# Turning the next expert's tokens two slabs earlier, and taking the low-part products last, in a float32 mixture-of-experts block

## The chip, the core and the metric

The kernel runs on one core of a Trainium2 chip. The time is the device time of one execution in microseconds, as the median of several runs; lower is better. PE is the matrix engine (PEld its weight loads), ACT the scalar engine, DVE the vector engine, POOL the general engine and SP the engine that issues most transfers.

## The reference

One layer of a streaming encoder on 1024 tokens of 1024 channels: a mixing half (gated DeltaNet heads beside sparse attention heads), then a routed mixture of experts. The change touches the experts alone. What they compute, cut to its core:

```python
logits = h @ router_w + router_b                  # 1024 tokens, 32 experts
top_val, top_idx = lax.top_k(logits, 4)
gate = softmax(top_val)
def block_ffn(xb, e):                             # the tokens of expert e
    act = clamped_swiglu(xb @ w1[e] + b1[e])      # 1024 x 2048
    return act @ w2[e] + b2[e]                    # 1024 x 1024
out[tok] += gate * block_ffn(h[tok], e)
```

All of it is float32.

## The kernel before

PE multiplies in a rounded float32 format. To keep float32 precision each operand is split: the high part is a cast to that format (ACT, L193), the low part is the operand less its high part (DVE, L194). A product is then three: high times high, high tokens times low weights, low tokens times high weights.

**Slabs and halves.** An expert's weights come in 12 slabs of 1 MB (s = 0 to 7 for the first matrix, 8 to 11 for the second), fetched by SP into a ring of nine. Each slab is split in two halves, so that an expert has 24 halves. They live in rings of nine tiles, `hi0` to `hi8` and `lo0` to `lo8`. The split runs five halves ahead of the slab that PE is at (`LOOK`).

**Tokens.** `gather` brings up to 128 tokens of an expert, chosen by an indirect transfer on POOL, into `xg`. `transpose_x` turns them: eight transposes on PE into two PSUM tiles, two copies on ACT for the high part of `xT` (L1623), two subtractions on DVE for the low part (L1624). The first block of an expert (`first`) takes 128 tokens; where an expert has more, a second block (`both`) takes the rest, either in full or, for 64 tokens or fewer, in a narrow form that puts high and low parts side by side (`half`, `transpose_half`, L1631 to L1634). Which of them runs is decided on the chip by two Ifs (L1532, L1533).

**Order.** The loop over experts goes through the slabs in groups of two (s0 = 0, 2, ..., 10). For a group the program names the splits, the first block's pieces with what follows them (`behind`: activation, turning of the activation into `aT`, the result `y`), and then the If with the second block's pieces. The tokens of expert e + 1 are turned in the group s0 = 10, between that group's splits and its pieces. A scheduling layer sets the final order of each engine between two Ifs: it may lift first-block work of later groups ahead of an If, and in fact lifts all of groups 8 and 10 ahead of the If of s0 = 8 but for eight products. An engine executes in that order; no instruction passes one that waits.

In this text a stretch is what stands between two Ifs, named after the If that ends it. Stretch 0 goes from the If of s0 = 10 of one expert to the If of s0 = 0 of the next, so that it holds the end of one expert and the beginning of another; stretch 2 goes from there to the If of s0 = 2, and so on to stretch 8. The splits of a stretch are four (eight in stretch 0), in the order of the halves.

**A piece** (`piece`, L1664) is one slab against one block: two halves of two 128-row steps each, three products per step, 12 in all, in the order high-high, high-low, low-high for each step.

Of the kernel before, what the change touches and what calls it, by code (L numbers as in the profile page):

```python
# [20 lines left out]
P = 128  # L21
# [6 lines left out]
NE = 32  # L28
# [108 lines left out]
class K:  # L137
# [1305 lines left out]
    def phase4(self):  # L1443
        nc, tc, A, pp = self.nc, self.tc, self.A, self.pp
        ET = mybir.EngineType
        with ExitStack() as es:
# [33 lines left out]
            def split(g):  # L1480
                if g < 2 * NE * NS:
                    self.split_ring(g)
                    if g % 2:
                        self.fetch(g // 2 + NR)
# [5 lines left out]
            def gather(b, e):  # L1490
                if e < NE:
                    self.gather(self.xg[b], ix(b, e))

            def path_of(e):
                return [nc.values_load(path[0:1, e:e + 1], engines=on, min_val=0, max_val=2)
                        for on in ((ET.PE, ET.Activation, ET.DVE), (ET.Pool,))]
# [8 lines left out]
            for e in range(NE):  # L1505
                several, pool = paths
                paths = path_of(e + 1) if e + 1 < NE else None
                pick = lambda h: self.sel[:, h, e:e + 1].to_broadcast([P, P])
                wt = lambda g: (self.hi[(2 * e * NS + g) % NW], self.lo[(2 * e * NS + g) % NW])
                first = Block(self, 0, P, self.xg[0], self.xT, pick, ga(0, e), self.y0)  # L1510
                xT1 = st.tile([P, 2, KD, P], F32R, name="xT1")
                both = Block(self, 1, P, self.xg[1], xT1, pick, ga(1, e), y1)
                half = both.half(lambda h: self.selh[:, h])

                for s0 in range(0, NS, GP):
                    group = range(s0, s0 + GP)
                    for s in group:
                        for part in range(2):
                            split(2 * (e * NS + s) + part + LOOK)
                    if s0 == 2:  # L1520
                        gather(1, e + 1)
                    if s0 == 10 and e + 1 < NE:
                        self.transpose_x(self.xg[0], self.xT)
                        gather(0, e + 2)
                    for s in group:
                        first.room(s)
                        first.piece(s, wt)
                        first.behind(s)

                    for s in group:  # L1530
                        both.room(s)
                    with tc.If(several > 0):  # L1532
                        with tc.If(several > 1) as many:  # L1533
                            if s0 == 0:
                                self.transpose_x(self.xg[1], xT1)
                            for s in group:
                                both.piece(s, wt)
                                both.behind(s)
                        with many.Else():
                            if s0 == 0:  # L1540
                                self.transpose_half(self.xg[1], half.X)
                                for h in range(2):
                                    nc.scalar.copy(self.selh[:, h, 0:64], self.sel[:, h, e:e + 1].to_broadcast([P, 64]))
                            for s in group:
                                half.piece(s, wt)
                                half.behind(s)
                self.add_rows(self.y0, ix(0, e), P)
                with tc.If(pool > 0):  # L1548
                    self.add_rows(y1, ix(1, e), P)
# [57 lines left out]
    def gather(self, xg, ix):  # L1607

        self.nc.gpsimd.indirect_dma_start(out=xg, out_offset=None, in_=self.dH[:, :],  # L1609
                                          in_offset=bass.IndirectOffsetOnAxis(ap=ix, axis=0), bounds_check=T - 1, oob_is_err=False)  # L1610
# [26 lines left out]
class Block:  # L1637
# [26 lines left out]
    def piece(self, s, wt):  # L1664
        nc, z = self.k.nc, self.z
        if s < 8:
            ps, X, h = self.rooms[s], self.X, s % 2
            if h == 0:
                c0 = 512 * (s // 2)
                nc.tensor.matmul(ps, self.pick(c0 // 1024), self.k.bias[:, c0 % 1024:c0 % 1024 + 512], start=True, stop=False,  # L1670
                                 skip_group_check=True)
            first = False
        else:
            ps, X, h = self.rooms[s], self.aT, (s - 8) // 2
            first = h == 0
        mm = lambda l, r, start, stop: nc.tensor.matmul(ps, l, r, start=start, stop=stop, skip_group_check=True)  # L1676
        for part in range(2):
            wh, wl = wt(2 * s + part)
            for j in range(2):
                k = 4 * h + 2 * part + j  # L1680
                begin, end = first and part == 0 and j == 0, h == 1 and part == 1 and j == 1
                if z == P:
                    mm(X[:, 0, k], wh[:, j], begin, False)
                    mm(X[:, 0, k], wl[:, j], False, False)
                    mm(X[:, 1, k], wh[:, j], False, end)
                else:
                    mm(X[:, k], wh[:, j], begin, False)
                    mm(X[:, k], wl[:, j], False, end)

    def behind(self, s):  # L1690

# [66 lines left out]
```

## Time and profile before

| | |
|---|---|
| time, median of 3 runs | 2689.1 us (2684.57 to 2692.34) |
| the profiled execution | 2686.3 us |
| its span, first to last instruction | 2684.6 us, 35831 instructions |
| PE busy | 2405.1 us (90%) |
| DVE busy | 1935.8 us (72%) |
| ACT busy | 1511.1 us (56%) |
| POOL busy | 599.2 us (22%) |
| read from memory, written | 534.89 MB, 54.57 MB |

The busy shares are averages over stages that differ. The experts begin about 1010 us after the start. PE's busy time contains pipelined products: one of 512 columns lasts about 0.39 us in the trace, while the next starts 0.23 us after it, so that the distance from start to start is what a product costs. The idle time in brackets in a timeline is counted from the end of the instruction before. "<-" names what ended it; PEq is PE's own sequencer.

### The profile page before, as it was taken

The page shows a single profiled execution, that of the slowest core. Times are in us where ns is not written, and L with a number is a line of the kernel's source. Part 1 is how long each engine was busy: PE and PEld are TensorE (multiplying, and loading weights), DVE is VectorE, ACT ScalarE, POOL GpSimd, SP SyncE. Part 2 cuts the span into 40 slices and gives each one's busy share as a digit, 9 for nine tenths or more (in the row PEclk, how much of TensorE's full clock was granted, in tenths as well). Part 3 has the DMA queues.
Part 4 walks back from the last instruction along what each step waited for, and adds up shares of the span by engine and source line. Part 5 has one row for each costly group of instructions (what it writes and reads, how often), then busy time and mean ns, then how long its engine had stood idle before and what let it go on. Part 6 is the DMA issues. An engine that isn't in the chain of part 4 may idle for free. (4 is left out here: it accounts for less than half of the span.)

```text
span 2684.6 us, 35831 instructions
## 1 busy us (share of the span) xinstructions
PE 2405.1 (90%) x11702; PEld 1914.4 (71%) x11702; DVE 1935.8 (72%) x3547; ACT 1511.1 (56%) x2449; POOL 599.2 (22%) x424
## 2 busy tenths in 40 slices
PE   5999989798897978999899989889999999999986
PEld 4877778787786756767677766666767777677765
DVE  6797896478875887886776676488888756775644
ACT  6558323267664325676665655467677646564533
POOL 0033321344532433121121120121221211121110
PEclk8999999889998979999999999999999999999998
DMA  8123345554414348896776675489999857784740
GB/s 316 48 80 133 110 164 195 166 135 126 116 47 180 120 157 299 315 336 240 272 281 239 232 284 195 170 295 335 334 328 329 315 181 265 252 308 183 268 146 12
DMA packets 144836, 570.66 MB, mean 213 GB/s; under 512 B 36820, under 2 KB 62452, under 8 KB 89252
## 3 DMA queue, kind: packets, MB, share of 16 engines
q1 hardware_dynamic: 111876, 496.33, 51.2%
q0 software_dynamic: 19792, 43.37, 6.4%
q10 hardware_dynamic: 12880, 27.30, 2.8%
q8 instruction: 159, 2.61, 0.4%
q14 instruction: 129, 1.06, 0.1%
HBM read 534.89 MB, written 54.57 MB: 220 GB/s over the span
## 5 line engine op out<-in xcount | busy, mean ns | idle before, releaser
L1676 PE MATMUL m<-hi,xT 128*128 128x512 f32 x2464 | 839.7, 406 | 90.3 <-DVE xT L1624 48.5
L1676 PEld LDWEIGHTS m<-hi,xT 128*128 128x128 f32 x2464 | 465.4, 193 | 243.3 <-DVE xT L1624 63.8
L194 DVE TENSOR_TENSOR lo<-raw,hi 128x1024 fp32r<-128x1024 f32 x436 | 509.8, 1220 | 104.0 <-ACT hi L193 102.3
L1676 PE MATMUL m<-lo,xT 128*128 128x512 f32 x1344 | 537.3, 400 | 0.1
L193 ACT CAST hi<-raw 128x1024 fp32r<-128x1024 f32 x436 | 428.9, 1046 | 114.4 <-PEq L1532 98.2
L194 DVE TENSOR_TENSOR lo<-yT,hi 128x1024 fp32r<-128x1024 f32 x340 | 398.0, 1220 | 68.4 <-ACT hi L193 68.4
L1676 PE MATMUL m<-hi,aT 128*128 128x512 f32 x1232 | 422.3, 406 | 6.6 <-ACT aT L1731 3.1
L193 ACT CAST hi<-yT 128x1024 fp32r<-128x1024 f32 x340 | 334.9, 1046 | 67.2 <-PEq L1532 61.1
L1609 POOL DMA_INDIRECT xg<-dH,L x63 | 79.7, 1265 | 999.3 <-PE tr L1621 963.1
L1676 PEld LDWEIGHTS m<-lo,xT 128*128 128x128 f32 x1344 | 257.8, 192 | 58.3 <-issue 0.8
L1676 PEld LDWEIGHTS m<-hi,aT 128*128 128x128 f32 x1232 | 226.9, 188 | 69.2 <-issue 12.2
L1613 POOL DMA_INDIRECT out_dram<-y,L x41 | 192.4, 4692 | 364.1 <-DVE y L1737 296.7
L1676 PE MATMUL m<-lo,aT 128*128 128x512 f32 x672 | 266.4, 396 | 7.3 <-DVE lo L194 7.3
L1717 ACT ACTIVATE act<-m,c 128x256 f32<-128x256 f32 x140 | 66.1, 472 | 245.1 <-PE m L1676 232.0
L200 PE MATMUL mm<-hTh,wh 128*128 128x512 f32 (+2 forms) x400 | 155.7, 389 | 2.0 <-ACT xpad L469 1.1
L202 PE MATMUL mm<-hTh,wl 128*128 128x512 f32 (+2 forms) x400 | 154.2, 385 | 0.0
L201 PE MATMUL mm<-hTl,wh 128*128 128x512 f32 (+2 forms) x400 | 154.2, 385 | 0.0
L1676 PEld LDWEIGHTS m<-lo,aT 128*128 128x128 f32 x672 | 126.5, 188 | 36.7 <-DVE lo L194 10.8
L1719 DVE TENSOR_SCALAR m<-m 128x256 f32<-128x256 f32 x140 | 59.8, 427 | 87.9 <-ACT act L1717 86.2
L1096 POOL TENSOR_TENSOR L<-Tb,mask 128x128 f32<-128x128 f32 (+3 forms) x64 | 85.9, 1342 | 159.1 <-PE tr L1135 116.8
L1708 DVE TENSOR_TENSOR y<-m,y 64x512 f32<-64x512 f32 x42 | 28.7, 682 | 127.4 <-ACT y L1707 127.4
L1707 ACT COPY y<-m 64x512 f32<-64x512 f32 x42 | 24.5, 582 | 151.8 <-PE m L1676 117.5
(461 smaller groups left out, 4171.0 us busy)
## 6 DMA issues: line engine op xcount, KB each, us to landing
raw<-in_w_dram SPq DMA_DIRECT2D x214, 1024.0 KB
yT<-in_w_dram SPq DMA_DIRECT2D x166, 1024.0 KB
raw<-in_mod_w_dram SPq DMA_DIRECT2D x24, 1024.0 KB
raw<-in_w_in_dram SPq DMA_DIRECT2D x16, 1024.0 KB
dU<-stage ACTq DMA_DIRECT2D x12, 512.0 KB
dT<-dF SPq DMA_DIRECT2D x8, 576.0 KB
x<-in_x_dram SPq DMA_DIRECT2D x8, 512.0 KB
dQK<-stage ACTq DMA_DIRECT2D x8, 512.0 KB
```

The costliest lines, as they stand in the source:

```text
L193: nc.scalar.copy(hi, raw)
L194: nc.vector.tensor_tensor(lo, raw, hi, op=ALU.subtract)
L200: nc.tensor.matmul(ps, xh(k), yh(k), start=(k == 0), stop=False)
L201: nc.tensor.matmul(ps, xh(k), yl(k), start=False, stop=False)
L202: nc.tensor.matmul(ps, xl(k), yh(k), start=False, stop=(k == n - 1))
L1096: nc.gpsimd.tensor_tensor(L[:, :n], Tb[:, t0:t0 + n], self.masks[b], op=ALU.add)
L1609: self.nc.gpsimd.indirect_dma_start(out=xg, out_offset=None, in_=self.dH[:, :], in_offset=bass.IndirectOffsetOnAxis(ap=ix, axis=0), bounds ...
L1613: self.nc.gpsimd.indirect_dma_start(out=self.out[:, :], out_offset=bass.IndirectOffsetOnAxis(ap=ix[:z], axis=0), in_=y[:z], in_offset=None ...
L1676: mm = lambda l, r, start, stop: nc.tensor.matmul(ps, l, r, start=start, stop=stop, skip_group_check=True)
L1708: k.nc.vector.tensor_tensor(u, ps[0:64], u, op=ALU.add)
L1717: nc.scalar.activation(r, ug, AF.Relu, bias=k.c7[:z, 0:1], scale=-1.0)
L1719: nc.vector.tensor_scalar(ul, ul, 7.0, -7.0, op0=ALU.min, op1=ALU.max)
```

## The change

Two edits. The turning of the next expert's tokens, with the gather for the expert after it, moves from the group s0 = 10, behind its splits, to the head of the group s0 = 8, ahead of that group's splits. And in a piece for 128 tokens the four products of a slab with the tokens' low parts come after the eight with the high parts; narrow blocks keep their order.

```diff
                 for s0 in range(0, NS, GP):
                     group = range(s0, s0 + GP)
+                    if s0 == 8 and e + 1 < NE:
+                        self.transpose_x(self.xg[0], self.xT)
+                        gather(0, e + 2)
                     for s in group:
                         for part in range(2):
                             split(2 * (e * NS + s) + part + LOOK)
                     if s0 == 2:
                         gather(1, e + 1)
-                    if s0 == 10 and e + 1 < NE:
-                        self.transpose_x(self.xg[0], self.xT)
-                        gather(0, e + 2)
                     for s in group:
...
-        for part in range(2):
-            wh, wl = wt(2 * s + part)
-            for j in range(2):
-                k = 4 * h + 2 * part + j
-                begin, end = first and part == 0 and j == 0, h == 1 and part == 1 and j == 1
-                if z == P:
-                    mm(X[:, 0, k], wh[:, j], begin, False)
-                    mm(X[:, 0, k], wl[:, j], False, False)
-                    mm(X[:, 1, k], wh[:, j], False, end)
-                else:
-                    mm(X[:, k], wh[:, j], begin, False)
-                    mm(X[:, k], wl[:, j], False, end)
+        ks = [(4 * h + 2 * part + j, *(t[:, j] for t in wt(2 * s + part)), first and part + j == 0, h + part + j == 3)
+              for part in range(2) for j in range(2)]
+        if z < P:
+            for k, wh, wl, begin, end in ks:
+                mm(X[:, k], wh, begin, False)
+                mm(X[:, k], wl, False, end)
+            return
+
+        for k, wh, wl, begin, end in ks:
+            mm(X[:, 0, k], wh, begin, False)
+            mm(X[:, 0, k], wl, False, False)
+        for k, wh, wl, begin, end in ks:
+            mm(X[:, 1, k], wh, False, end)
```

The scheduling layer moves more than the diff says. The pieces below are of one expert whose ring starts at `hi0`, so that `hi8` is the first split of stretch 6, `hi0` the second, and `hi3`, `hi4`, `hi5` the first three of stretch 8.

ACT in stretch 8 (the If of s0 = 6 behind it), before:

```order
L193 CAST hi3_8874<-raw1_8868 128x1024
L193 CAST hi4_8875<-raw2_8869 128x1024
L193 CAST hi5_8876<-raw2_8869 128x1024
L193 CAST hi6_8877<-raw3_8870 128x1024
L1731 CAST aT0_16778<-tr_17280 128x256
```

and of the change:

```order
L193 CAST hi3_8874<-raw1_8868 128x1024
L1623 CAST xT_10447<-tr_17244 128x512
L1623 CAST xT_10447<-tr_17251 128x512
L193 CAST hi4_8875<-raw2_8869 128x1024
L193 CAST hi5_8876<-raw2_8869 128x1024
L193 CAST hi6_8877<-raw3_8870 128x1024
L1732 CAST aT0_16778<-tr_17297 128x256
```

The two copies of the tokens stand behind the first split of stretch 8; before they stood behind the fourth of stretch 0. DVE has its two subtractions at the same place.

PE at the head of stretch 8, before (m0 are the first block's sums, m1 the second's, aT0 the first block's turned activation, act0 the activation itself):

```order
L1532 UNCONDITIONAL_BRANCH
L1676 MATMUL m0_17267<-hi0_8871,aT0_16778 128x512 x2
L1676 MATMUL m0_17267<-lo0_8865,aT0_16778 128x512
L1676 MATMUL m0_17267<-hi0_8871,aT0_16778 128x512
L1676 MATMUL m0_17267<-hi1_8872,aT0_16778 128x512
L1676 MATMUL m0_17267<-lo1_8866,aT0_16778 128x512
L1676 MATMUL m0_17267<-hi1_8872,aT0_16778 128x512 x2
L1676 MATMUL m0_17267<-lo1_8866,aT0_16778 128x512
L1676 MATMUL m0_17267<-hi1_8872,aT0_16778 128x512
L1727 MATMUL tr_17280<-ident_60,act0_17156 128x128 x2
L1676 MATMUL m0_17254<-hi2_8873,aT0_16778 128x512
L1676 MATMUL m0_17254<-lo2_8879,aT0_16778 128x512
```

and of the change:

```order
L1532 UNCONDITIONAL_BRANCH
L1621 MATMUL tr_17244<-ident_60,xg0_10391 128x128 x4
L1621 MATMUL tr_17251<-ident_60,xg0_10391 128x128 x4
L1676 MATMUL m0_17271<-lo2_8879,aT0_16778 128x512
L1676 MATMUL m0_17271<-hi2_8873,aT0_16778 128x512
L1676 MATMUL m0_17271<-lo2_8879,aT0_16778 128x512
L1670 MATMUL m0_17484<-bias_9602,sel_9603 128x512
L1728 MATMUL tr_17297<-ident_60,act0_17156 128x128 x2
L1676 MATMUL m0_17284<-hi4_8875,aT0_16778 128x512
L1676 MATMUL m0_17284<-lo4_8881,aT0_16778 128x512
L1676 MATMUL m0_17284<-hi4_8875,aT0_16778 128x512
L1676 MATMUL m0_17271<-hi3_8874,aT0_16778 128x512
```

The products of `hi0` and `hi1` have moved ahead of the If of s0 = 6. `hi4`, a split of this stretch, stands behind the transposes, three products and a bias row; before it stood behind 16 products.

PE at the head of stretch 6, before:

```order
L1532 UNCONDITIONAL_BRANCH
L1676 MATMUL m0_17142<-hi4_8875,xT_10447 128x512
L1676 MATMUL m0_17142<-hi5_8876,xT_10447 128x512
L1676 MATMUL m0_17142<-lo5_8882,xT_10447 128x512
L1676 MATMUL m0_17142<-hi5_8876,xT_10447 128x512 x2
L1676 MATMUL m0_17142<-lo5_8882,xT_10447 128x512
L1676 MATMUL m0_17142<-hi5_8876,xT_10447 128x512
L1676 MATMUL m0_17142<-hi6_8877,xT_10447 128x512
L1676 MATMUL m0_17142<-lo6_8883,xT_10447 128x512
L1676 MATMUL m0_17142<-hi6_8877,xT_10447 128x512 x2
L1676 MATMUL m0_17142<-lo6_8883,xT_10447 128x512
L1676 MATMUL m0_17142<-hi6_8877,xT_10447 128x512
```

and of the change:

```order
L1532 UNCONDITIONAL_BRANCH
L1676 MATMUL m0_17142<-hi5_8876,xT_10447 128x512
L1676 MATMUL m0_17142<-hi6_8877,xT_10447 128x512 x2
L1728 MATMUL tr_17173<-ident_60,act0_17044 128x128 x2
L1676 MATMUL m0_17271<-hi7_8878,aT0_16778 128x512
L1676 MATMUL m0_17271<-lo7_8884,aT0_16778 128x512
L1676 MATMUL m0_17271<-hi7_8878,aT0_16778 128x512
L1676 MATMUL m0_17271<-lo7_8884,aT0_16778 128x512
L1676 MATMUL m0_17271<-hi8_10444,aT0_16778 128x512
L1676 MATMUL m0_17284<-hi0_8871,aT0_16778 128x512
L1676 MATMUL m0_17271<-lo8_10445,aT0_16778 128x512
L1676 MATMUL m0_17271<-hi8_10444,aT0_16778 128x512
```

`hi8` and `hi0`, splits of this stretch, stand behind seven products and two transposes; before, `hi8` stood behind 19 products, of which the piece shows the first 13.

## Rows read from the trace of the kernel before

**Rows 1.** Waits of the whole span: us in total, times, longest us
```profile
...
PE m L1676 <- DVE xT L1624: 48.5, 31, 2.6
...
PE m L1676 <- ACT xT L1623: 26.3, 27, 2.1
```

**Rows 2.** The tile xT: count, ns min/median/max, first and last start
```profile
...
L1624 DVE TENSOR_TENSOR xT<-tr,xT x70: 669/682/692, 1012.2 to 2593.4; 128x512 fp32r<-128x512 f32 x70
L1633 ACT CAST xT<-tr x7: 578/585/587, 1232.3 to 2601.8; 128x512 fp32r<-128x512 f32 x7
```

**Rows 3.** Windows: length, busy (count) by engine, clock, DMA share, GB/s
```profile
...
1441.00:1486.00 45.00, 40.63 (x168) 30.77 (x167) 36.63 (x44) 29.38 (x39) 9.40 (x4) 0.92 0.84 290
1831.00:2117.00 286.00, 263.75 (x1149) 201.45 (x1148) 240.15 (x280) 201.66 (x266) 59.82 (x21) 1.00 0.92 333
```

**Rows 4.** Timeline of PE, start of an expert: start, us, instruction, [idle <-releaser]
```profile
...
1872.63 1.07 PE L1621 MATMUL tr<-ident,xg 128*128 128x128 f32 x8 [0.71 <-PEq L1532]
1873.45 0.72 PE L1676 MATMUL m<-hi,aT 128*128 128x512 f32 x2
...
1876.46 0.50 PE L1676 MATMUL m<-hi,xT 128*128 128x512 f32 x1 [0.67 <-ACT xT L1623]
...
1878.41 0.73 PE L1676 MATMUL m<-hi,xT 128*128 128x512 f32 x2 [1.21 <-DVE xT L1624]
```

**Rows 5.** Timeline of ACT, the same stretch
```profile
...
1875.84 1.06 ACT L1623 CAST xT<-tr 128x512 fp32r<-128x512 f32 x2
```

**Rows 6.** Timeline of DVE, the same stretch
```profile
...
1877.67 1.28 DVE L1624 TENSOR_TENSOR xT<-tr,xT 128x512 fp32r<-128x512 f32 x2
1878.87 1.40 DVE L1737 SCALAR_TENSOR_TENSOR y<-m,L,g2b 128x512 f32<-128x512 f32 x2
```

**Rows 7.** Timeline of PE, an expert's second products, no second block
```profile
...
1913.48 0.74 PE L1621 MATMUL tr<-ident,xg 128*128 128x128 f32 x5 [0.71 <-PEq L1532]
```

**Rows 8.** Timeline of ACT, the same stretch
```profile
...
1906.21 1.05 ACT L193 CAST hi<-yT 128x1024 fp32r<-128x1024 f32 x1 [1.95 <-PEq L1532]
1907.16 2.94 ACT L193 CAST hi<-raw 128x1024 fp32r<-128x1024 f32 x3
```

**Rows 9.** Timeline of DVE, the same stretch
```profile
...
1907.29 1.23 DVE L194 TENSOR_TENSOR lo<-yT,hi 128x1024 fp32r<-128x1024 f32 x1 [1.25 <-ACT hi L193]
1908.43 3.49 DVE L194 TENSOR_TENSOR lo<-raw,hi 128x1024 fp32r<-128x1024 f32 x3
```

**Rows 10.** Timeline of PE, an expert with a narrow second block
```profile
...
1414.61 0.73 PE L1676 MATMUL m<-hi,xT 128*128 128x512 f32 x2
```

**Rows 11.** Timeline of ACT, the same stretch
```profile
...
1416.78 2.93 ACT L193 CAST hi<-yT 128x1024 fp32r<-128x1024 f32 x3
```

**Rows 12.** Timeline of DVE, the same stretch
```profile
...
1417.85 2.36 DVE L194 TENSOR_TENSOR lo<-yT,hi 128x1024 fp32r<-128x1024 f32 x2 [0.52 <-ACT hi L193]
```

**Rows 13.** Timeline of PE, that expert, behind its first If
```profile
...
1391.59 0.63 PE L1676 MATMUL m<-hi,xT 128*128 128x512 f32 x2
```

**Rows 14.** Timeline of DVE, the same stretch
```profile
...
1396.33 0.42 DVE L1720 SCALAR_TENSOR_TENSOR act<-m,act 128x256 f32<-128x256 f32 x1
```

**Rows 15.** Timeline of PE, that expert's second products
```profile
...
1425.50 0.73 PE L1676 MATMUL m<-hi,aT 128*128 128x512 f32 x2
...
1431.15 0.49 PE L1676 MATMUL m<-lo,aT 128*128 128x512 f32 x1 [0.94 <-DVE lo L194]
1431.86 0.50 PE L1676 MATMUL m<-hi,aT 128*128 128x512 f32 x1 [0.22 <-ACT aT L1731]
```

**Rows 16.** Timeline of PE, start of the expert behind it
```profile
...
1441.74 1.03 PE L1621 MATMUL tr<-ident,xg 128*128 128x128 f32 x8
...
1447.01 0.80 PE L1676 MATMUL m<-hi,xT 128*128 128x512 f32 x1 [2.14 <-ACT xT L1623]
...
1449.80 1.22 PE L1676 MATMUL m<-hi,xT 128*128 128x512 f32 x2 [1.56 <-DVE xT L1624]
```

**Rows 17.** Timeline of DVE, the same stretch
```profile
...
1444.53 4.61 DVE L194 TENSOR_TENSOR lo<-raw,hi 128x1024 fp32r<-128x1024 f32 x4
```

## The prediction

> **What bounds the kernel now.** The experts begin at 1012 of the span's 2684.6 us [rows 2] and run to its end. I read first the windows: over the seven experts from 1831 to 2117 PE is busy 263.75 of 286 us with 1149 instructions, at clock 1.00 and a DMA share of 0.92 [rows 3]. So PE sets the pace, at 0.23 us from one instruction to the next, and an expert without second block takes 40.85 us (1872.63 to 1913.48, [rows 4, 7]). Then the waits: PE idles 48.5 us for the low parts of the next expert's tokens and 26.3 for their high parts, nearly once per expert each [rows 1]. The timelines show why. The turned tokens stand on ACT and DVE behind four splits, and PE has only eight products and a bias row to run before it needs them [rows 4 to 6]. Start to start, at 0.23 a product and some 0.08 more after a stall, this costs 0.86 us (1876.46 instead of 1875.60) and 1.41 (1878.41 instead of 1877.00): 2.2 us per expert. Behind an expert with a narrow second block the waits are 2.14 and 1.56, the clock of the next 45.0 us is 0.92 [rows 3, 16], and that expert takes 4.1 us more than the 40.85, so the same place costs 6.3 there, some 2.1 of it clock.
>
> There are 7 narrow second blocks (x7 of L1633) and 3 full ones (70 halves of tokens turned, 64 of them for first blocks) [rows 2]; 22 experts have none. The last expert is a narrow one and turns no further tokens.
>
> A fact that decides below: ACT and DVE start a stretch's four splits only when PE has left the If ahead of it ("<-PEq L1532" in [rows 8]). Without second block ACT starts with PE; behind a narrow block it starts 2.17 us after PE (1414.61 to 1416.78) and DVE 3.24 [rows 10 to 12], because it still finishes that block's activation.
>
> **The change, part by part.** Nothing is added: the same 8 transposes, 2 copies, 2 subtractions, the same 12 products per piece, one gather. The waits change place.
>
> *The turn at stretch 0 goes.* It takes away the 2.2 (or 6.3) us. What is late next there: DVE now runs one result and four low parts first. Without second block the first low part of the next weights is ready about 3.4 us into the stretch, PE asks at 3.5 (seven products left, then four): no wait. Behind a narrow block DVE is free at 1444.53 [rows 17]; one result (two take 1.40, [rows 6]) and a low part, 0.70 + 1.23, end at 1446.5, PE (from 1441.74, eleven products, one more) asks at 1444.7: a wait of 1.8 stays.
>
> *The turn at stretch 8, no second block.* Let ACT's first split begin at 0 [rows 8]. PE's transposes take 0.82 (1872.63 to 1873.45, [rows 4]). ACT: first split, then at 0.95 the two copies, 1.06 together [rows 5], so the second split ends at 2.01 + 1.05 = 3.06. DVE: first low part at 1.08, next start 1.14 later [rows 9], then the two token low parts, 1.28 [rows 6], so the second low part ends at 2.22 + 1.28 + 1.23 = 4.73. PE: 0.84 after the transposes, three products and a bias row 0.92, two transposes 0.25: at 2.0 it asks for the second split (hi4 in the order): wait 1.06. One product later, at 3.3, it asks for lo4: wait 1.44. Together 2.5 us where the trace has no wait at all on splits. The two matmul orders together show it: PE asks for the first half of the last slab (hi4) before the second half of the one before it (hi3), and nothing behind a waiting product passes it. All the products of the piece and the second block's If queue behind it. Bounds: nothing (PE has no such wait now) and 4.7 (the narrow case below). I take 2.5, since every duration in it is a row.
>
> *Low parts last, and the later Ifs.* The order hoists more products ahead of each If and asks each slab's second half two products earlier. So a stretch begins with fewer products of old weights, and PE reaches the stretch's own first split sooner: in stretch 6 after 7 products and two transposes instead of 19 products. Without second block that just fits (asked at about 2.0, ready at 1.1), except stretch 2, where the transposes of the activations stand behind 13 products instead of 22 and wait about 0.25. Behind a narrow block it doesn't fit. Stretch 6: asked at 1.95, ready at 2.17 + 1.05 = 3.22; the next split asked 0.23 later, ready at 4.17; the low part at 4.47: together 2.1. Stretch 4: asked at 2.65, ready 3.22; low part asked at 3.5, ready 4.47: 1.6. Stretch 2: the activation is ready at 1396.75, 5.16 after PE's start [rows 13, 14]; asked at 3.1: 2.1. Stretch 8: ACT's copies wait for PE's transposes, which need DVE's tail of the If; second split ends about 5.7, second low part about 7.0, asked at 2.3: 4.7. Now in stretch 8 lo4 is the 18th product, due at 4.3 and run at 5.65, and the next wait adds 0.4 [rows 15]: 1.8.
>
> *What costs nothing.* The gather of expert e + 2 goes out some 10 us earlier on POOL, ahead of the rows to be added, and both have an expert's time to land. SP's slab transfers are issued behind the splits; in stretch 8 the second split is 1.1 us later, which nine slabs of lead cover at a DMA share of 0.92; without that cover each would cost its 1.1. The order of additions in a piece changes no duration.
>
> **The sum**, in us against the profiled 2686.3 (span 2684.6, 1.7 around it):
> - 22 experts without second block: -2.2 + 0.25 + 2.5 = +0.5 each, +11.
> - 6 narrow ones: new 2.1 + 1.6 + 2.1 + 4.7 + 1.8 = 12.3, old 1.8 + 6.3 = 8.1: +4.2 each, +25. The last one, without turn: 2.1 + 1.6 + 2.1, about +6.
> - 3 full ones: between nothing and the narrow 4.2; nearer to nothing, since ACT has no copy to make there: +1 each, +3.
>
> +45, so 2731. The profiled execution lies 2.8 under the median of the runs, inside their spread of 7.8; I leave it at 2731.
>
> **Rivals.**
> - *The waits vanish.* The tokens are ready early and PE meets no new wait: 22 x 2.2 + 6 x 6.3 + 3 x 4 (estimate between the two) = 98 less, 2588. For it: the 75 us in [rows 1]. Against: [rows 8, 9] give the splits no room, and at 38.6 us an expert the DMA share 0.92 becomes 0.97. It decides if PE reaches hi4 and lo4 of stretch 8 more than 2.5 us later than I count. Chance 0.17.
> - *It cancels.* PE's longer stretches let DVE catch up, the narrow experts lose half of 4.2 and the others gain half a us: within 8 us of 2686. Chance 0.15.
> - *The clock falls at the new place.* In stretch 8 two waits come close together, behind transposes and four products. Where the clock falls now it costs 2.1 us more than the waits; at the 28 turns of experts with a narrow block or none this is 59 more: 2790. For it: [rows 3], 0.92 behind waits of 2.14 and 1.56. Against: the seven experts from 1831 wait 0.67 and 1.21 behind the same transposes at 1.00. Chance 0.12.
>
> The Trainium skill (TensorE: Matmul & The Clock Gate, "Part 4: PE-mode transpose") says that transposes don't count as busy time for the clock as products do. By that rule the head of stretch 8 would look idler than a row of products, and the time would go to the third rival's 2790; by the rows at 1.00, where the same transposes stand ahead of the waits, it stays at 2731.
>
> **How the numbers follow.** Forecast 0.56, rivals 0.17, 0.15, 0.12. About 0.3% (8 us) is what a measurement can tell from no change here. Slower: forecast and third rival, 0.68; same 0.15; faster 0.17. The likeliest case alone runs from 2700 (no second block -0.5 each, narrow +3 and +6, full 0) to 2755 (+1.5, +4.2 and +6, +1). The range goes down to 2678, the lower end of the second rival, and up to 2790, the third.
>
> **What would show it.** Right: waits of PE for xT gone, new ones "<-ACT hi" and "<-DVE lo" of about 1.1 and 1.4 at L1676 in aT products, once per expert, an expert without second block at 41 to 41.5 us, a narrow one 3 to 5 us longer than now with its successor. ACT's and DVE's busy times unchanged. Wrong: periods under 40.5 us, or waits on splits that stay under 1 us per expert; then PE's place in the order was misjudged. A clock under 1.00 in the windows of experts without second block would be the third rival.

## The result and the profile after

The change makes the kernel slower: 2757.3 us median (2749.34 to 2761.77, 4 runs) against 2687.5 (the kernel before, by now 4 runs), a ratio of 1.0255 with a 95% interval of 1.0225 to 1.0284. The forecast was 2731, in the range 2678 to 2790. The profiled execution of after is the lowest of its runs (2749.3 us, span 2747.6), so that the two profiles differ by 63.0 us of span where the medians differ by 69.7.

The waits of PE over the whole span of after (us in total, times, longest), which answer to [rows 1]:

```profile
PE m L1676 <- DVE lo L194: 47.2, 44, 1.8
PE tr L1728 <- DVE act L1721: 30.7, 10, 9.2
PE tr L1728 <- DVE xT L1624: 29.7, 31, 1.8
PE m L1676 <- ACT hi L193: 17.9, 26, 3.0
```

The 48.5 and 26.3 us for xT in products are gone but for 0.4. In their place PE waits for low and high parts of splits, and its transposes of the activations (L1728) wait for the subtractions of xT and, longer than before, for the activations themselves (30.7 us against 11.3).

To place the loss I took each expert from ACT's first split of its stretch 0 to that of the next expert. An expert without second block lasts 40.86 us before and 40.91 after (medians of the same seven experts): nothing gained, nothing lost. The six narrow experts with their successors cost 50.3 us more, 8.4 each; the three full ones 4.4 together; the last expert 8.7. That makes up the 63 (the rest cancels within half a us).

The windows of after show the same. First row: seven experts without second block, against [rows 3]; then stretches 2, 4, 6 and 8 of the narrow expert that begins at 1377.5; last, stretch 2 of another narrow expert. Columns as in [rows 3].

```profile
1872.50:2158.80 286.30, 263.81 (x1148) 200.75 (x1148) 240.09 (x280) 200.28 (x267) 59.21 (x21) 1.00 0.90 331
...
1397.10:1412.32 15.22, 13.06 (x52) 9.99 (x51) 7.80 (x13) 6.79 (x12) 0.00 (x0) 0.89 0.35 138
1412.32:1424.98 12.66, 11.38 (x48) 8.09 (x46) 7.13 (x11) 6.69 (x12) 0.00 (x0) 1.00 0.45 167
1424.98:1439.89 14.91, 12.29 (x49) 9.29 (x49) 7.13 (x11) 6.68 (x12) 0.00 (x0) 0.89 0.37 141
1439.89:1457.60 17.71, 14.82 (x59) 11.18 (x58) 7.55 (x10) 6.45 (x11) 1.00 (x1) 0.90 0.42 150
1518.80:1532.40 13.60, 11.45 (x52) 8.78 (x51) 7.80 (x13) 6.74 (x12) 0.00 (x0) 1.00 0.42 157
```

The same four stretches of the same expert in the kernel before:

```profile
1394.09:1405.66 11.57, 11.49 (x51) 8.85 (x50) 7.80 (x13) 6.80 (x12) 0.00 (x0) 1.00 0.48 182
1405.66:1416.75 11.09, 11.09 (x50) 8.73 (x49) 7.13 (x11) 6.69 (x12) 0.00 (x0) 1.00 0.51 191
1416.75:1427.64 10.89, 10.89 (x49) 8.53 (x48) 7.13 (x11) 6.68 (x12) 0.00 (x0) 1.00 0.50 194
1427.64:1442.43 14.79, 13.63 (x61) 10.08 (x61) 6.36 (x8) 5.47 (x9) 0.00 (x0) 1.00 0.38 143
```

With the same busy time on DVE in stretches 2 to 6, they are 3.65, 1.57, 4.02 and 2.92 us longer, and the clock is below 1.00 in three of them.

Stretch 8 of an expert without second block in after, PE (start, us, instruction, idle time and releaser), which answers to [rows 4, 7]:

```profile
1905.76 1.06 PE L1621 MATMUL tr<-ident,xg 128*128 128x128 f32 x8 [0.30 <-PEq L1532]
...
1908.55 0.44 PE L1728 MATMUL tr<-ident,act 128*128 128x128 f32 x2 [0.79 <-DVE xT L1624]
1908.74 0.48 PE L1676 MATMUL m<-hi,aT 128*128 128x512 f32 x1
1910.28 0.50 PE L1676 MATMUL m<-lo,aT 128*128 128x512 f32 x1 [1.05 <-DVE lo L194]
```

ACT and DVE in that stretch, which answer to [rows 5, 6, 8, 9]:

```profile
1905.59 1.05 ACT L193 CAST hi<-yT 128x1024 fp32r<-128x1024 f32 x1 [2.25 <-PEq L1532]
1906.54 1.07 ACT L1623 CAST xT<-tr 128x512 fp32r<-128x512 f32 x2
1907.50 2.95 ACT L193 CAST hi<-yT 128x1024 fp32r<-128x1024 f32 x3
```

```profile
1906.67 1.23 DVE L194 TENSOR_TENSOR lo<-yT,hi 128x1024 fp32r<-128x1024 f32 x1 [1.55 <-ACT hi L193]
1907.81 1.28 DVE L1624 TENSOR_TENSOR xT<-tr,xT 128x512 fp32r<-128x512 f32 x2
1909.01 3.49 DVE L194 TENSOR_TENSOR lo<-yT,hi 128x1024 fp32r<-128x1024 f32 x3
```

The activations' transposes need one of two PSUM tiles (`tr`), which the subtractions release; so PE stops there, ahead of the product of the second split. That split ends at about 1908.55 (1907.50 + 1.05), the moment at which PE goes on: without the tile, the split would have held it about as long.

Stretch 2 of the narrow expert in after, PE, which answers to [rows 13, 14]. Behind the wait a product follows the last by 0.43 us, not 0.23, the lower of the clock's two levels (1.2 instead of 2.4 GHz):

```profile
1397.35 0.39 PE L1676 MATMUL m<-hi,xT 128*128 128x512 f32 x1
1399.90 0.47 PE L1728 MATMUL tr<-ident,act 128*128 128x128 f32 x2 [2.16 <-DVE act L1721]
...
1400.60 0.63 PE L1676 MATMUL m<-hi,xT 128*128 128x512 f32 x1
1401.02 0.63 PE L1676 MATMUL m<-lo,xT 128*128 128x512 f32 x1
```

The same place in another narrow expert of the same execution, behind the same wait:

```profile
1518.98 0.39 PE L1676 MATMUL m<-hi,xT 128*128 128x512 f32 x1
1521.52 0.41 PE L1728 MATMUL tr<-ident,act 128*128 128x128 f32 x2 [2.15 <-DVE act L1721]
...
1522.00 0.39 PE L1676 MATMUL m<-hi,xT 128*128 128x512 f32 x1
1522.23 0.39 PE L1676 MATMUL m<-lo,xT 128*128 128x512 f32 x1
```

Here the clock stays up, and the stretch lasts 13.60 us instead of 15.22: one fall of the clock costs 1.6 us.

### The profile page after: what moved, and what is told of

The parts are those of the page before. It is cut to its first block, busy times and chain, and to the rows that moved or that the text cites. A ratio compares the mean times of both kernels' runs of the same rounds, so it can differ in the third digit from the quotient of the medians.

```text
span 2747.6 us, 35638 instructions
## 1 busy us (share of the span) xinstructions
PE 2421.4 (88%) x11702; PEld 1916.7 (70%) x11702; DVE 1933.7 (70%) x3547; ACT 1507.1 (55%) x2449; POOL 601.5 (22%) x424
## 3 DMA queue, kind: packets, MB, share of 16 engines
q14 instruction: 130, 1.06, 0.1%
## 4 chain that ended last, share of the span: by engine, by line
issue 55%; PE 8%; POOL 6%; DMA 5%; DVE 4%; ACT 1%; another core or an unknown queue 1%; POOLq 1%; SPq 0%; ACTq 0%; DVEq 0%
POOL xg L1609 3%; POOL out_dram L1613 2%; DMA out_dram<-y,L 1%; PE tr L1145 1%; DMA dL<-pair,rdest 1%; DMA xg<-dH,L 1%; PE big L202 1%; PE big L200 1%; PE big L201 1%; DVE Xb L931 1%; DMA raw<-in_w_out_dram 1%; PE tr L1135 1%; PE lg L1118 1%; DVE tb L929 1%
## 5 line engine op out<-in xcount | busy, mean ns | idle before, releaser
L1676 PE MATMUL m<-hi,xT 128*128 128x512 f32 x2464 | 829.5, 400 | 13.7 <-DVE xT L1634 6.8
L1676 PE MATMUL m<-lo,xT 128*128 128x512 f32 x1344 | 543.3, 405 | 23.9 <-DVE lo L194 17.5
L1676 PE MATMUL m<-hi,aT 128*128 128x512 f32 x1232 | 430.9, 414 | 35.7 <-ACT hi L193 15.1
L1676 PEld LDWEIGHTS m<-hi,aT 128*128 128x128 f32 x1232 | 237.6, 194 | 108.5 <-ACT hi L193 24.9
L1676 PE MATMUL m<-lo,aT 128*128 128x512 f32 x672 | 280.1, 417 | 29.7 <-DVE lo L194 29.7
L1609 POOL DMA_INDIRECT xg<-dH,L x63 | 86.6, 1375 | 755.1 <-PE tr L1621 702.5
```

## The experiments

All times are medians; ratios are against the kernel before on the same chip. "hi8" counts the first-block products that stand ahead of the first product of stretch 6's own first split in PE's order (the transposes of activations beside them). "next stretch" says that this product stands only behind the next If, and an empty field that it was not counted. "Plain" is the median of the seven experts without second block that begin at 1831 in the kernel before; "narrow" the mean of four narrow experts each with its successor.

| kernel | us | ratio, 95% interval | hi8 | plain | narrow |
|---|---|---|---|---|---|
| before | 2687.5 | 1 | 19 | 40.86 | 112.9 |
| the change | 2757.3 | 1.0255 (1.0225 to 1.0284) | 7 | 40.91 | 120.7 |
| turn_only | 2778.3 | 1.0335 (1.0303 to 1.0367) | 5 | 41.80 | 123.0 |
| low_last_only | 2716.8 | 1.0112 (1.0084 to 1.0140) | 12 | 40.90 | 115.8 |
| turn10_ahead | 2742.9 | 1.0190 (1.0156 to 1.0225) | 6 | 40.60 | 119.5 |
| after_trm0 | 2642.6 | 0.9831 (0.9805 to 0.9857) | next stretch | 40.68 | 107.9 |
| turn_only_trm0 | 2638.1 | 0.9814 (0.9791 to 0.9837) | next stretch | 40.69 | 108.4 |
| before_res | 2664.1 | 0.9901 (0.9883 to 0.9919) | | 40.23 | 110.0 |
| best_res | 2679.3 | 0.9952 (0.9937 to 0.9966) | next stretch | 43.18 | 107.3 |
| best_short | 2627.4 | 0.9763 (0.9739 to 0.9786) | | 39.17 | 106.7 |
| best_clamp | 2652.1 | 0.9854 (0.9821 to 0.9888) | next stretch | 40.70 | 109.9 |

**Which edit does it: turn_only, low_last_only, turn10_ahead.**

turn_only is the change without the new product order; low_last_only is the change with the turn at its old place:

```diff
-                    if s0 == 8 and e + 1 < NE:
-                        self.transpose_x(self.xg[0], self.xT)
-                        gather(0, e + 2)
...
                     if s0 == 2:
                         gather(1, e + 1)
+                    if s0 == 10 and e + 1 < NE:
+                        self.transpose_x(self.xg[0], self.xT)
+                        gather(0, e + 2)
```

> The turn of the tokens at the head of s0 = 8, products in the old order. Theory A (the moved turn is what lets the order put first-block products ahead of every If, so that PE meets the splits early; the product order has no part in the loss): 2740 to 2765 us, narrow experts with their successor 7 to 9 us longer than before, waits on splits in stretches 4, 6 and 8 as in the changed kernel. Theory B (the prediction's wording: low parts last is what asks for the splits earlier in stretches 2 to 6, the moved turn costs in stretch 8 alone): 2675 to 2695, narrow experts with their successor 0 to 2 us shorter than before.

> The turn at its old place behind the splits of s0 = 10, low parts last in a piece. Theory A: 2685 to 2710, since in the order of this kernel hi8 of stretch 6 stands behind 12 products and two transposes; the waits for xT at stretch 0 shrink from 2.2 to some 1.3 us (low parts are asked eight products later) and one of about 0.9 on the low part of the second split of stretch 8 comes in. Theory B: 2735 to 2755, with waits on splits in narrow experts' stretches 4 and 6.

turn10_ahead is the kernel before with those three lines at the head of its group s0 = 10, ahead of the splits:

> The turn stays in the group s0 = 10 but goes to its head, ahead of the splits; products in the old order. Theory A (the order moves because PE no longer waits for xT, wherever the turn goes): the products stand as far ahead of the Ifs as in the changed kernel, narrow experts lose 6 to 8 us with their successor, experts without second block gain 0 to 1: 2710 to 2735. Theory B: no wait for xT, no new waits in stretches 2 to 6: 2650 to 2670.

The moved turn alone costs 3.35%, more than the whole change and more than either theory had (2740 to 2765 at most); low parts last alone costs 1.1%, and beside the moved turn it gives 21 us back (2778 to 2757). So Theory A is right on what moves the products ahead of the Ifs, and wrong in that the product order has no part: low_last_only missed both ranges. turn10_ahead leaves the turn in stretch 0 and still has its products as far ahead (column hi8), at 2743 somewhat above the forecast of 2710 to 2735. So it is enough that the turn leaves the place behind the four splits; where it goes matters less. Stretch 6 of the same narrow expert, low_last_only first, then turn_only:

```profile
1420.67:1433.11 12.44, 11.68 (x51) 8.48 (x49) 7.13 (x11) 6.69 (x12) 0.00 (x0) 1.00 0.47 171
```

```profile
1428.73:1443.40 14.67, 12.07 (x49) 9.27 (x49) 7.14 (x11) 6.30 (x11) 0.00 (x0) 0.88 0.38 144
```

With 12 products ahead of `hi8` it lasts 12.44 us, with 5 it lasts 14.67 and the clock falls; before, with 19, it was 10.89. Of the 2.2 us between the two rows the clock can explain some 1.7 (14.67 times the missing 0.12).

In turn10_ahead an expert without second block meets no wait of PE for xT (behind the six narrow ones a wait of 1.3 us is left), and two in stretch 8:

```profile
1944.92 0.50 PE L1676 MATMUL m<-hi,aT 128*128 128x512 f32 x1 [0.41 <-ACT hi L193]
1946.38 0.50 PE L1676 MATMUL m<-lo,aT 128*128 128x512 f32 x1 [0.95 <-DVE lo L194]
```

Together 1.36 us of idle time against 1.88 in [rows 4], and the plain expert is 0.26 us shorter. The waits change their place at almost equal length a third time.

turn10_ahead also answers a rival, that the two PSUM tiles which the tokens' and the activations' transposes share are what costs. They are shared here too, no transpose of activations waits for a subtraction of xT (29.7 us in after), and the kernel still loses 1.9%.

**Own tiles for the tokens: after_trm0, turn_only_trm0.**

```diff
         for q in range(2):
-            pt = self.ptr.tile([P, 512], F32, name="tr")
+            pt = self.pb[0].tile([P, 512], F32, name="m0")
```

> The changed kernel, with the eight transposes of the tokens written into two of the first block's own three PSUM tiles (m0) instead of the two that the activations' transposes use as well. In its order the copies of xT stand at the end of stretch 6, the subtractions at the head of stretch 8, the first split of a stretch again behind 10 or more products. Theory A (what costs is how early PE meets splits): no wait for xT and none on splits in stretch 8, an expert without second block at 38.6 to 39.5 us, narrow ones as before or better: 2600 to 2645. Theory B (low parts last costs by itself): experts without second block at 40 to 41 and narrow ones 5 us or more above before: 2700 or more.

> The turn at the head of s0 = 8 with its transposes in two tiles of m0, products in the old order. Its order stands at the Ifs within two products of that with low parts last. Theory A: the product order hardly matters once PE asks late enough: 2630 to 2660, against 2642.6 with low parts last. Theory B (low parts last is a gain of its own, as 2757 against 2778 with the turn at the same place suggests): 2665 to 2690.

The edit changes the order as well: the tokens are turned at the end of stretch 6, their copies stand behind all splits there, and no stretch asks for its own splits early. Both kernels beat before by 1.7% and 1.9%. The stretches 2 to 8 of the narrow expert in after_trm0:

```profile
1389.83:1401.16 11.33, 11.33 (x51) 8.94 (x50) 7.80 (x13) 7.22 (x13) 0.00 (x0) 1.00 0.49 186
1401.16:1412.23 11.07, 11.07 (x50) 8.75 (x49) 7.13 (x11) 6.70 (x12) 0.00 (x0) 1.00 0.50 192
1412.23:1421.46 9.23, 9.23 (x46) 7.37 (x45) 7.13 (x11) 7.64 (x14) 1.14 (x1) 1.00 0.65 232
1421.46:1435.62 14.16, 13.85 (x61) 10.56 (x60) 7.47 (x10) 5.61 (x10) 0.00 (x0) 1.00 0.49 184
```

PE is busy almost throughout at clock 1.00. That is the loss undone, with the changed turn and the changed product order both in the kernel; the product order by itself is worth less than can be told here (the intervals of 0.9831 and 0.9814 overlap). How much of the gain is the new order and how much the tiles' own release is not separated. The time fell in narrow experts as Theory A expects. In plain ones it did not: 40.68, where A expected 38.6 to 39.5, though no wait for xT or a split is left.

**Splits six halves ahead: after_look6, after_trm0_look6, before_look6.**

```diff
-LOOK = NW - 2 * GP
+LOOK = 6
```

> The changed kernel with the splits six halves ahead of PE instead of five (LOOK = 6). In its order the third split of stretch 8 stands behind 28 instructions of PE, and the activations' transposes there behind the tokens' and ten products; stretches 4 and 6 ask none of their own first splits before 20 products. Theory A (the loss is how soon PE asks for a split behind an If): waits on splits go in stretches 4 to 8, an expert without second block takes 39 to 40 us, a narrow one with its successor 4 to 8 us less than before: 2600 to 2650. Theory B (the loss is in the two PSUM tiles that the tokens' transposes share with the activations', and own tiles gave the gain): those are still shared here, so 2720 or more.

> Both: transposes of the tokens in m0 tiles, and splits six halves ahead. Theory A: little is left to gain on splits; what PE waits for in the own-tiles run is the release of an m0 tile by DVE behind the If of s0 = 0 (3.15 us after a narrow expert), and that stays: 2615 to 2645. If the splits' lead is worth something by itself: under 2615.

> The kernel before with the splits six halves ahead. The tokens are turned at stretch 0 behind three splits instead of four, so the waits for xT shrink by about 0.9 us per expert at most, and more behind narrow experts if the clock stays up: 2650 to 2690 by Theory A. If the lead of the splits were worthless: 2685 to 2692.

They took 2716.8 (1.0106), 2665.9 (0.9914) and 2672.7 us (0.9943). The edit was a poor one: a ring of nine holds five halves of lead and a group of four, so the last split of a group now lands in the tile of the group's first half, ahead of its products; these products use the newer half and must wait for it. The waits of PE in after_look6 show that new wait, up to 15.1 us long:

```profile
PE m L1676 <- DVE lo L194: 96.2, 34, 15.1
```

So these three tell nothing of either theory, though before_look6 fell in its range; the other two missed theirs.

**What holds a plain expert: best_res, best_short, before_res, best_clamp.** Six kernels with different waits on PE had plain experts of 40.6 to 40.9 us (turn_only, at 41.80, has a third wait on splits of 0.45 us, and the clock at 0.96 in three of its seven). In [rows 3] DVE is busy 34.3 us per expert (240.15 / 7). What it idles goes to one wait, the first split behind each If; the kernel before, six such experts:

```profile
DVE lo L194 <- ACT hi L193: 38.4, 30, 1.7
```

34.3 and 38.4 / 6 = 6.4 make 40.7. The sum by itself shows nothing, since the busy and idle time of any engine add up to the length; what suggests Theory D is that DVE's idle time has this one cause: ACT's first split and then DVE's chain, from If to If, last as long as the expert. In stretch 0 of the kernel before, DVE works without a gap from 1873.12 to 1884.80 (its rows between these two are in [rows 6] and one split at 1876.53), while PE's waits for xT end at 1878.41:

```profile
1873.12 3.50 DVE L194 TENSOR_TENSOR lo<-yT,hi 128x1024 fp32r<-128x1024 f32 x3 [1.71 <-ACT hi L193]
1880.18 4.62 DVE L194 TENSOR_TENSOR lo<-raw,hi 128x1024 fp32r<-128x1024 f32 x4
```

And where PE has no wait for a token or a split, as in turn_only_trm0, it waits for DVE at the Ifs, here in six experts, with 5.4 us more of the same at L1670:

```profile
PE m L1676 <- DVEq L1532: 10.4, 6, 1.7
```

Three edits on turn_only_trm0 and one on before:

```diff
+        if self.b == 0:
+            k.nc.scalar.activation(self.y[:z, c], self.rooms[10 + q][:z], AF.Copy, scale=self.ga[:z])
+            k.nc.gpsimd.tensor_tensor(self.y[:z, c], self.y[:z, c], k.g2b[:z, c], op=ALU.mult)
+            return
```

> The kernel with the turn at s0 = 8, own tiles and the old product order (2638.0 us), with the first block's two results per expert taken off DVE: scaled by the gate on ACT, multiplied by g2b on POOL. PE's order is the same to the instruction. Theory D (an expert without second block lasts as long as DVE's chain: its busy time and, behind each If, the wait for ACT's first split; the 1.4 us of results come off it): 39.2 to 39.6 us for such an expert instead of 40.7, 2590 to 2605 in all. Theory P (PE's products and its Ifs set the pace): 2632 to 2640.

> The kernel before with the first block's results on ACT and POOL as in best_res. Theory D for the kernel before too: 1.2 to 1.4 us less per expert without second block, 2645 to 2660. If instead the waits for xT hold the kernel before (they stay as they are, since the results stand behind the subtractions on DVE): 2680 to 2692.

```diff
-        self.split(self.raw[g // 2 % NR][:, 2 * (g % 2):2 * (g % 2) + 2], self.hi[g % NW], self.lo[g % NW])
+        raw, hi, lo = self.raw[g // 2 % NR][:, 2 * (g % 2):2 * (g % 2) + 2], self.hi[g % NW], self.lo[g % NW]
+        self.nc.scalar.copy(hi, raw)
+        j = slice(0, 1 if g % 4 == 3 else 2)
+        self.nc.vector.tensor_tensor(lo[:, j], raw[:, j], hi[:, j], op=ALU.subtract)
```

> The same kernel (2638.0 us) with the low part of every fourth half computed for one of its two 128-row steps only, so that the other keeps old values: six subtractions per expert of about 0.6 us less, 3.7 us of DVE's time; ACT, PE and the transfers do the same work. Theory D: experts without second block fall until PE holds them, 38.9 to 39.5 us (the 40.85 of before less the 1.9 that PE waited), 2580 to 2600 in all. Theory P: 2630 to 2645.

```diff
-        nc.vector.tensor_scalar(ul, ul, 7.0, -7.0, op0=ALU.min, op1=ALU.max)
-        nc.vector.scalar_tensor_tensor(r, ul, 1.0, r, op0=ALU.add, op1=ALU.mult)
+        if self.b:
+            nc.vector.tensor_scalar(ul, ul, 7.0, -7.0, op0=ALU.min, op1=ALU.max)
+        else:
+            nc.scalar.activation(ul, ul, AF.Relu, bias=k.c7[:z, 0:1], scale=-1.0)
+            nc.scalar.activation(ul, ul, AF.Relu, bias=k.c7[:z, 2:3], scale=-1.0)
+        nc.vector.scalar_tensor_tensor(r, ul, 1.0 if self.b else -6.0, r, op0=ALU.add, op1=ALU.mult)
```

> The same kernel (2638.0 us) with the first block's clamp of the activations' linear half moved from DVE (one operation of 0.43 us, four times per expert) to ACT (two, by Relu twice, with the constant of the next operation on DVE changed from 1 to -6 to match). PE's order is the same to the instruction; nothing goes to POOL. Theory D (DVE's chain holds an expert without second block): four times 0.34 us from start to start, 1.4 us, come off: 39.2 to 39.6 us for such an expert, 2600 to 2615 in all. Theory P: 2634 to 2642, or more if the activations, later by two operations on ACT, are waited for.

best_short, which leaves out a part of the low parts, has the plain expert where Theory D puts it: 39.17 us, in the range 38.9 to 39.5. Six of them, turn_only_trm0 first, then best_short:

```profile
1849.20:2093.30 244.10, 222.92 (x984) 174.50 (x984) 206.87 (x240) 173.59 (x229) 50.86 (x18) 1.00 0.93 335
```

```profile
1852.70:2087.70 235.00, 223.09 (x984) 174.61 (x984) 190.01 (x240) 173.52 (x228) 33.75 (x18) 1.00 0.93 348
```

The same 984 instructions and 223 us on PE, the same on ACT, 16.9 us less on DVE, and 9.1 us less in all. PE's waits for DVE at the Ifs fall from 15.8 us to 3.6. But the scheduling layer moved the order of ACT and DVE in the plain expert as well (in stretch 0 ACT has seven splits behind the If where turn_only_trm0 has eight), so the 1.5 us per expert belong to the shorter chain and its new order together. What the run does show is that PE's work fits into 39.17 us. Its total of 2627 missed the forecast of 2580 to 2600: the order of the narrow experts moved too, and two in a row (from 1579 on) lost 6.5 and 8.3 us.

The other two on turn_only_trm0 suggest that DVE alone is too narrow a name. best_clamp took four operations off DVE and put eight on ACT, and the plain expert did not move (40.70); by its time alone (2652) this is what Theory P foretold. DVE now waits longer for ACT's splits, 34.5 us in six experts against 26.4; turn_only_trm0 first, then best_clamp:

```profile
DVE lo L194 <- ACT hi L193: 26.4, 23, 1.5
```

```profile
DVE lo L194 <- ACT hi L193: 34.5, 30, 1.6
```

Against Theory P, PE still waits for DVE at the Ifs as long as in turn_only_trm0 (10.3 and 5.3 us against 10.4 and 5.4), so DVE came there as late as before, with less work of its own:

```profile
PE m L1677 <- DVEq L1533: 10.3, 6, 1.7
```

best_res even lost: 43.18 us. The multiplications on POOL and the subtractions of DVE beside them slowed each other; DVE of turn_only_trm0, then DVE and POOL of best_res, at the same place of an expert:

```profile
1850.31 3.50 DVE L194 TENSOR_TENSOR lo<-yT,hi 128x1024 fp32r<-128x1024 f32 x3 [1.51 <-ACT hi L193]
```

```profile
1863.04 5.71 DVE L194 TENSOR_TENSOR lo<-raw,hi 128x1024 fp32r<-128x1024 f32 x3
```

```profile
1863.11 4.56 POOL L1739 TENSOR_TENSOR y<-y,g2b 128x512 f32<-128x512 f32 x2 [12.13 <-ACT y L1738]
```

Three subtractions take 5.71 us instead of 3.50, which eats the 1.4 us that the results had taken on DVE and leaves 0.8 of loss. The rest is the clock: of the seven plain experts three took 41.6 to 41.8 us at clock 1.00, and four 43.2 to 43.6 with a clock of 0.96. before_res gained 0.6 us per plain expert, half of its forecast, and its 2664 lie between the two ranges. What fits all four runs is that the alternation of ACT and DVE between the Ifs holds a plain expert: work taken out of it shortened the expert, work passed on within it did not. No run shortens ACT's share alone or keeps the order fixed while it shortens DVE's.

## Why the prediction was right, and where it was not

**Direction and cause: right.** The waits for xT go, new waits on splits come, and the narrow experts pay the most. The waits of the narrow expert at 1377.5 stand beside their forecasts: stretch 2 2.16 (2.1), stretch 4 0.47 + 0.76 (1.6), stretch 6 1.15 + 0.45 (2.1), stretch 8 1.07 + 1.84 + 1.05 (4.7), stretch 0 1.76 (1.8). Together 10.7 for 12.3.

**The term that was mis-sized: +4.2 for a narrow expert.** It measured 8.4. The waits were rather over-counted, so the miss is the clock. The sum took away what the fall of the clock had cost at the old place (2.1 of the 6.3) and put none behind the new waits. But behind the waits of stretches 2, 6 and 8 the windows stand at 0.89, 0.89 and 0.90, and one such fall costs 1.6 us. 10.7 less the old 8.1 is 2.6; three falls make up to 4.8; nine restarts at some 0.1 us bring it near the 8.8 that this expert and its successor lost.

All six bear that out. What the clock can have cost in an expert is at most its length times one less its granted clock, taken from the trace; for each narrow expert with its successor, in us:

| begins in after at | longer by | clock's cost, before | clock's cost, after |
|---|---|---|---|
| 1217.1 | 6.6 | 3.4 | 3.4 |
| 1377.5 | 8.8 | 3.4 | 5.1 |
| 1499.3 | 7.5 | 1.7 | 3.4 |
| 1619.4, two narrow ones and a successor | 19.2 | 6.8 | 15.4 |
| 2279.2 | 8.2 | 3.4 | 5.1 |
| all | 50.3 | 18.8 | 32.4 |

The clock took 13.6 us more, 2.3 per narrow expert, where the sum had 2.1 less. Without it a narrow expert is 6.1 us longer; without its clock the forecast is 12.3 less 6.0, 6.3. So the waits together were sized well, and by this account the miss of 4.2 is the clock: the sum had it fall less often, and it fell more often.

The third rival had this mechanism, and it acted at six of its 28 places. In stretch 8 of the narrow experts, where it put the falls, the clock did fall in five of six (0.90 or 0.91). But it fell in their stretches 2 and 6 as well, and at only one turn of the 22 experts without second block. The one from 1830.2 to 1872.5 took 42.3 us at 0.96, with the same waits of 0.80 and 1.06 us as the seven behind it, which stayed at 1.00 [first window of after]. The Trainium skill (TensorE: Matmul & The Clock Gate, "Part 4: PE-mode transpose") says that transposes don't count as busy for the clock as products do. That made the head of stretch 8 the suspect; seven experts in a row at 1.00 behind the same transposes, and falls in stretches 2 and 6, which have none of the tokens' transposes, do not bear it out as what decides. What decides whether the clock falls behind a wait of 2.15 or 2.16 us, or behind the two of stretch 8, stays open: both cases stand above.

**The step on low parts last: right in its waits, wrong in its owner.** The prediction laid the earlier asking in stretches 2 to 6 to the product order. turn_only has it without that order, and more of it (5 products ahead of `hi8`, not 7); the product order without the turn has less (12). What the scheduling layer puts ahead of an If had changed because the turn left the place behind the splits; why the layer does so was not tried.

**Plain experts: +0.5 forecast, 0.05 measured, for a reason that was missed.** The new waits are 0.79 and 1.05, not 1.06 and 1.44, the first is at the activations' transposes, for a PSUM tile that the sum did not look at, and the 0.25 for stretch 2 is not in the trace. Beyond that the sum took the 2.2 us of [rows 4] as a gain to be had and PE as what sets the pace. best_short shows otherwise: PE does the same work in 39.17 us. PE's two microseconds of idle time were, by this reading, largely slack beside ACT and DVE, and this is also why the first rival's 2588 was not there: without a wait on splits, after_trm0 still needs 40.68 us for a plain expert.

**The small terms.** Full experts +1.4, +1.3 and +1.6 (forecast +1 each), which is luck in part: in the kernel before each has one fall of the clock (1.7 us) that after lacks, so that the rest is about +3, nearer to the narrow case than to nothing. The last expert +8.7 (forecast +6), of which the clock can explain 2.0. Gather, transfers and the order of additions cost nothing that shows: the DMA share of the plain experts is 0.90.

## What to carry to other kernels

Where a scheduling layer sets the order, moving one step changes how far all the others are lifted ahead of the next branch; read the new order of the whole loop, and ask at each branch which operand of the other side is wanted first and when that side starts. A wait in the profile is a gain only if the engine that waits sets the pace: add up the other engines' busy time and their waits behind each branch before a wait is priced. When a wait is moved, price the clock behind its new place too.

## What the runs showed of the hardware

- A subtraction on DVE with both operands in SBUF (128x1024, median 1.22 us) took up to 2.35 us while POOL multiplied two SBUF operands, and POOL's 128x512 took 2.30 us there against 1.35 in before_res (medians), where less of it fell beside DVE. The Trainium skill (SBUF — State Buffer, "Who interferes with whom") says that a DVE instruction with two SBUF inputs contends with a GpSimd instruction that reads SBUF; these runs agree.
- Two waits of 2.15 and 2.16 us at the same place of the same program left the granted clock at 1.00 once and let it fall once; the products behind the second followed each other by 0.43 us instead of 0.23, for 1.6 us in all. Two waits of 0.80 and 1.06 us, close together, left it at 1.00 in seven experts in a row and let it fall in the one ahead of them (0.96).
